# The recurrence over chunks of an RWKV-7 layer: products of one tile shape issued side by side, and longer pauses around them

## The chip, the core and the metric

One core of one Trainium2 chip runs the whole program. The metric is the device time of one execution in microseconds (us). Three executions of the kernel before are given: 1921.01, 1919.91 and 1916.69 us, median 1919.91 us.

A core has engines that run side by side, each of them in its own instruction order: TensorE (PE) multiplies matrices from SBUF into PSUM banks, VectorE (DVE) and ScalarE (ACT) work on SBUF and PSUM, GpSimd (POOL) does a few small things here, and SyncE (SP) starts the DMAs. They wait for each other by semaphores.

## The reference

Two layers follow each other, each as x + RMSNorm(mixer(RMSNorm(x))), with 256 tokens of 2048 features, all in float32. Layer 0 mixes by an RG-LRU and an mLSTM. Layer 1, where the change is, mixes by RWKV-7:

```python
u = h @ w_in                                  # 2048 -> 4 * 4096: r, k, v, z
...
def step(S, inp):                             # one token, per head of 64 x 64
    r_t, w_t, k_t, v_t, kk_t, a_t = inp
    sa = jnp.einsum('bhvk,bhk->bhv', S, -kk_t)
    S = (S * w_t[:, :, None, :] + sa[..., None] * (kk_t * a_t)[:, :, None, :]
         + v_t[..., None] * k_t[:, :, None, :])
    return S, jnp.einsum('bhvk,bhk->bhv', S, r_t)
...
y = head_norm(y, H, RWKV_GN_EPS, gn_g, gn_b) + bonus
return (y * jax.nn.silu(z)) @ w_out           # 4096 -> 2048
```

There are 64 heads of 64 features. The kernel cuts the 256 tokens into 4 chunks of 64, so that each chunk is a set of small matrix products and only the state S passes from chunk to chunk.

## The kernel before, in words

**Two kinds of TensorE work.** The bulk is the four projections, w_in and w_out of both layers. Each float32 weight is split into a high part (`whi`, an ACT copy) and a rest (`wlo`, a DVE subtraction), and so is the activation (`hh`, `hl`). A piece of an input projection (`in_mms`, line 220) is 24 products of 128x128 by 128x256 into the `gb` banks: 16 with `whi`, 8 with `wlo`; eight pieces make one projection of 512 columns. I call these the stream. All that the mixers need besides, in the `mb` banks, is small.

**Layer 1 by groups.** The loop at line 1144 takes the 64 heads in 8 groups of 8 heads (index g). For each group it issues four projections in the order k, r, z, v. The mixer's steps of the group run beside them, and reach over into the projections of the next group: the recurrence of group g runs during k and r of group g + 1.

**What sets the order.** TensorE runs in program order (`InOrder`, line 101; its instructions carry lines 116 and 119). The class `Weave` (line 57) writes that order: after every 4 stream products it adds 0.44 to a counter (`tick`), and emits from four lanes the steps whose time has come. A mixer is a Python generator; `yield w` says how much of the counter passes before its lane goes on. After a step that issued TensorE products the next step waits for 0.4 more, so that between two steps' products there are at least 4 stream products. A lane holds generators in a queue: lane 0 `blocks` and `inverse`, lane 1 `scores`, `values`, `recur`, `final`, lane 2 the first `norm`, lane 3 `decay` and `keys`. `drain` empties a lane's generator at a point where its result is needed, with few or no stream products between its steps. `Behind` (line 122) holds ACT's and DVE's instructions behind the weight splits that were emitted ahead of them, so ACT and DVE, too, work in the order in which the steps were emitted.

**The steps that matter here.**

- `shifted` and `keys` (line 836): after the k projection ACT and DVE make `kt`, ACT squares it into `sq` (four ACTIVATEs), and TensorE sums it per head (`mb<-cs,sq`, 8 products 128x2). DVE then makes `Gn` and `kP`, ACT and DVE make `BK` (8 times xx, zz, and a product of both).
- `blocks` (line 876): 32 products 64x64, `mb<-AR,BK`, which read all of `BK`; then `inverse` (line 935), a long substitution on DVE (`tf`, `Tb`), ending in 32x32 products (`ZT,Aab` and `TT,ZT`).
- `scores` (line 900): DVE makes the right half of `AR` from `rt`; TensorE makes, for f = 0 to 3, 8 products of 64x128 tiles (`mb<-AR,BK`) and 4 transposes (`mb<-cs,BK`); DVE evacuates them to `At`, ACT to `BKt`.
- `recur` (line 1028), for c = 0 to 3: `wb` = At (A part) times `UV`, ACT copies it to `Ws`; `ub` = inverse times `Ws` (`mb<-Ws,TT`, 64x64 tiles), DVE scales it into `UV`; `sb` = `BKt` times `UV` (`mb<-UV,BKt`, 128x64 tiles), DVE updates the state `Sn`, ACT copies it to the next chunk's slot of `UV`; then the outputs `Yb` = At (R part) times `UV` (`mb<-UV,At`, 128x64) plus, for c > 0, `Rc` times the old state (`mb<-Sn,Rc`, 64x64). `wb` and the first part of `Yb` read alike in the profile, `mb<-UV,At`. Each of these is a set of 8 products.
- `norm` (line 1112): ACT copies `Yb` to `Yn` and squares it, DVE and POOL make the rate, DVE multiplies. It runs for chunks 0 and 1 in lane 2 as soon as chunk 1's outputs are issued, and for chunks 2 and 3 at the end of `recur`, which then turns the result with 8 transposes (`mb<-cs,Yn`) into `yT` and adds the bonus on DVE. `final` (line 1132) multiplies it with the gate (`zt`, DVE).

The `mb` banks are four. A step that allocates one waits until the last reader of that bank is done.

Of the kernel before, what the change touches and what calls it, by code (L numbers as in the profile page):

```python
# [13 lines left out]
P = 128  # L14
# [12 lines left out]
# columns of the packed per-feature vectors: (name, tiles)  # L27
# [18 lines left out]
# columns of the constant array  # L46
# [10 lines left out]
class Weave:  # L57
    """Steps of the mixers, emitted between the products of the projections. A step yields the amount of
    products that come before its lane goes on."""
# [41 lines left out]
class InOrder:  # L101
    """The tensor engine, issuing in the order of the program."""
# [19 lines left out]
class Behind:  # L122
    """An engine whose instructions follow, in its own order, the splits of the weights emitted before them."""
# [20 lines left out]
def two_layers(ctx, tc, x, gpost, cst, selc, v0, v1, w_in0, w_out0, w_in1, w_out1, lruw, qkvw,  # L144
# [36 lines left out]
    def keep_warm(n, b):  # L181
        """Products that keep the clock of the tensor engine up while it waits; nothing reads them."""
        for _ in range(n):
            pe.matmul(b, lhsT=ones[:, 0:P], rhs=ones, start=True, stop=True)
# [15 lines left out]
    # ---------------------------------------------------------------- products  # L200
    def split_w(raw, w=512, into=None):
        """Weights to their high part and the rest."""
# [17 lines left out]
    def in_mms(banks, hi, lo, pc, h, nft, tick):  # L220
        """One piece (two k-tiles) of an input projection: first what needs the high parts of the weights alone."""
# [17 lines left out]
    def in_proj(wsrc, h):  # L239
        """512 columns of an input projection, features on partitions: two banks of two tiles."""  # L240
        banks = [gbank(), gbank()]
        for pc in range(8):
            in_mms(banks, *split_w(load_w(wsrc[pc])), pc, h, 4, 0.44)
        return banks
# [10 lines left out]
    def out_proj(wsrc, get_y, evac, tick, finish, after, room=None):  # L255
        """Output projection, tokens on partitions; get_y(g): the two parts of k-tiles 4g..4g+3. The last
        pieces of the last chunk go token tile by token tile, so that what follows the first is covered."""
# [49 lines left out]
    # ---------------------------------------------------------------- norms, tokens on partitions  # L307
    def rstd(ss):
        """ss [P, 4]: partial sums of squares of a token tile -> [P, 1]."""
# [10 lines left out]
    def scale(ss, pool_):  # L320
        """diag(rstd) of a token tile: transposes by products with it are scaled."""
# [4 lines left out]
    def to_features(xs, dg, g, warm):  # L326
        """Four tiles [P, 2, 512] of tokens, scaled by dg and g, to the two parts of h."""
        banks = {}
# [34 lines left out]
    def log1p_of(e, tmp):  # L363
        """log(1 + e), 0 <= e <= 1, as 2 atanh(e / (2 + e)); tmp: three tiles like e."""
# [12 lines left out]
    def silu2(banks, sz):  # L377
        """sz = 2 silu of two banks."""
# [6 lines left out]
    def residual(layer, tile_of):  # L385
        """The evacuation of out_proj: sums of squares, and the products with the post-norm's weights."""
# [17 lines left out]
    # ================================================================ layer 0  # L404
    with ExitStack() as l0:
# [35 lines left out]
        # small tables  # L441
# [37 lines left out]
        # ------------------------------------------------------------ mLSTM inputs  # L479
# [6 lines left out]
        def mlstm_in(c, xm):  # L486
# [43 lines left out]
            # both gates: two column tiles side by side, summed at the end  # L530
# [104 lines left out]
        # ------------------------------------------------------------ RG-LRU  # L635
# [70 lines left out]
        def room():  # L706
            """Parts of the weights in the place of what the heads have done with."""
# [18 lines left out]
    # ================================================================ layer 1  # L726
    with ExitStack() as l1:
# [19 lines left out]
        # derived per-feature vectors; the halves of the heads' partitions swap B and K  # L747
# [19 lines left out]
        def loras():  # L767
            """The first halves of the two loras: the token shift is taken after the product."""
# [35 lines left out]
        def decay(g, st):  # L804
            """What depends on the loras: the decay within chunks of 64 tokens, and the rate."""
# [481 lines left out]
```

## Time and profile before

| what | value |
|---|---|
| median of three executions | 1919.91 us (1916.69 to 1921.01) |
| span of the profiled execution, first to last instruction | 1912.7 us |
| PE busy | 1883.4 us, 98% of the span |
| PE weight loads busy | 1747.9 us, 91% |
| DVE busy | 1395.3 us, 73% |
| ACT busy | 1044.1 us, 55% |
| DMA, mean | 157 GB/s |
| mean granted TensorE clock | 0.997 |

The profile gives no time of its own for the profiled execution beside its span; the median of the runs lies 7.2 us above the span, the lowest run 4.0 us. One group of layer 1 takes about 131 us, which one reads from the same step of two neighbouring groups.

The rows of a timeline hold the start in us from the start of the span, the length in us, engine, line, operation, output<-inputs, TensorE's tile, the shape, how many instructions the row joins, and in brackets the idle time in front of it with what ended it. A float32 product shows as two records, so a set of 8 products is a row of x16. Lengths of neighbouring products overlap, so what a product costs is read from one start to the next.

### The profile page before, as it was taken

To read this page: it belongs to the slowest core of one execution; us is meant where nothing else is said; L and a number is where in the kernel's file an instruction comes from. 1 tells how busy PE (TensorE), PEld (TensorE's weight loads), DVE (VectorE), ACT (ScalarE), POOL (GpSimd) and SP (SyncE) were. 2 spreads that over 40 slices of the span, in tenths; PEclk is the share of its full clock that TensorE was granted. 3 is DMA by queue.
4 is the path that set the end of the run, shared out by engine and by line. 5 is a ranking of instruction groups with operands and counts; after the bars stand their busy time and mean duration, and the time that the engine had idled before them with its cause. 6 is when DMAs were issued, how large, how long until landed. Compare 5 with 4: busy or idle time off the path is not lost.

```text
span 1912.7 us, 39517 instructions
## 1 busy us (share of the span) xinstructions
PE 1883.4 (98%) x16498; PEld 1747.9 (91%) x16498; DVE 1395.3 (73%) x2302; ACT 1044.1 (55%) x1609; POOL 60.4 (3%) x84
## 2 busy tenths in 40 slices
PE   8999999999999999999999999999999999999998
PEld 7999999999888899989999999999999999997886
DVE  5667777757554569969689689597796896895544
ACT  5444666645444546555565555655655655555442
POOL 0000000000000100000000000000000000000000
PEclk9999999999999999999999999999999999999999
DMA  7433545455666444434444434344344443356664
GB/s 250 142 133 111 177 162 169 155 171 194 215 208 195 168 147 135 152 118 144 133 136 138 133 130 155 111 147 149 113 150 139 136 136 131 122 187 203 211 202 156
DMA packets 86947, 299.63 MB, mean 157 GB/s; under 512 B 9576, under 2 KB 12392, under 8 KB 86768
## 3 DMA queue, kind: packets, MB, share of 16 engines
q1 hardware_dynamic: 86768, 297.11, 47.2%
q8 instruction: 129, 2.11, 0.5%
q14 instruction: 50, 0.41, 0.1%
HBM read 289.20 MB, written 7.86 MB: 155 GB/s over the span
## 4 chain that ended last, share of the span: by engine, by line
PE 93%; DVE 4%; ACT 1%; issue 1%; DMA 0%; POOL 0%; SPq 0%; DVEq 0%; POOLq 0%; ACTq 0%
PE gb L116 75%; PE mb L116 17%; DVE wlo L132 2%; PE mb L119 1%; DVE wb L132 1%; ACT whi L132 1%; DMA xq<-in_x_dram 0%; DVE rt L132 0%; DVE Tb L132 0%; DVE tf L132 0%; DVE Ab L132 0%; DVE yT L132 0%; ACT ZT L132 0%; ACT vt L132 0%; DVE At L132 0%
## 5 line engine op out<-in xcount | busy, mean ns | idle before, releaser
L132 DVE TENSOR_TENSOR wlo<-raw,whi 128x1024 fp32r<-128x1024 f32 x509 | 619.9, 1219 | 338.0 <-ACT whi L132 304.5
L132 ACT CAST whi<-raw 128x1024 fp32r<-128x1024 f32 x509 | 532.6, 1048 | 557.3 <-PE gb L116 512.3
L116 PE MATMUL gb<-hh,whi 128*128 128x256 f32 x3120 | 790.5, 289 | 2.8 <-ACT whi L132 2.8
L116 PE MATMUL gb<-hl,whi 128*128 128x256 f32 x3120 | 770.6, 283 | 0.0
L116 PEld LDWEIGHTS gb<-hh,whi 128*128 128x128 f32 x3120 | 596.7, 191 | 13.6 <-ACT whi L132 3.7
L116 PEld LDWEIGHTS gb<-hl,whi 128*128 128x128 f32 x3120 | 597.5, 192 | 0.8
L116 PE MATMUL gb<-hh,wlo 128*128 128x256 f32 x3120 | 453.5, 286 | 0.0
L116 PEld LDWEIGHTS gb<-hh,wlo 128*128 128x128 f32 x3120 | 404.9, 191 | 4.2 <-issue 0.7
L116 PE MATMUL gb<-whi,yl 128*128 128x512 f32 x500 | 136.9, 392 | 0.5 <-DVE yl L132 0.5
L116 PE MATMUL gb<-whi,yh 128*128 128x512 f32 x500 | 136.5, 392 | 0.0
L116 PE MATMUL gb<-wlo,yh 128*128 128x512 f32 x500 | 135.7, 390 | 0.0
L116 PEld LDWEIGHTS gb<-whi,yl 128*128 128x128 f32 x500 | 93.2, 188 | 20.4 <-DVE yl L132 0.9
L116 PEld LDWEIGHTS gb<-wlo,yh 128*128 128x128 f32 x500 | 93.5, 188 | 19.8
L116 PEld LDWEIGHTS gb<-whi,yh 128*128 128x128 f32 x500 | 93.0, 188 | 19.3
L132 DVE TENSOR_TENSOR Tb<-Tb,tf 64x31 f32<-64x31 f32 (+15 forms) x248 | 82.6, 333 | 6.1
L132 DVE TENSOR_TENSOR tf<-Ab,Tb 64x31 f32<-64x31 f32 (+15 forms) x248 | 81.9, 330 | 4.5
L116 PE MATMUL mb<-AR,BK 64*128 64x128 f32 (+1 forms) x1024 | 58.0, 253 | 7.0 <-DVE AR L132 6.0
L116 PEld LDWEIGHTS mb<-AR,BK 64*128 64x128 f32 (+1 forms) x1024 | 50.2, 161 | 13.3 <-PE gb L116 7.1
L132 DVE TENSOR_TENSOR UV<-mb,Gn 64x256 f32<-64x256 f32 x64 | 26.9, 421 | 34.5 <-PE mb L116 33.4
L132 ACT ACTIVATE zz<-kP,dv 128x256 f32<-128x256 f32 x64 | 32.3, 505 | 22.9 <-DVE kP L132 12.4
L116 PEld LDWEIGHTS mb<-UV,At 128*64 128x64 f32 (+1 forms) x1024 | 35.0, 137 | 10.3 <-issue 2.5
L1125 POOL TENSOR_TENSOR vr<-vr,mhalf 128x8 f32<-128x8 f32 x16 | 28.3, 1771 | 499.4 <-DVE vr L132 499.4
(258 smaller groups left out, 1855.9 us busy)
## 6 DMA issues: line engine op xcount, KB each, us to landing
raw<-in_w_in_dram SPq DMA_DIRECT2D x384, 512.0 KB, 3.3
raw<-in_w_out_dram SPq DMA_DIRECT2D x128, 512.0 KB, 4.3
y1d<-zt SPq DMA_DIRECT2D x7, 512.0 KB, 3.9
yraw<-y1d SPq DMA_DIRECT2D x7, 512.0 KB, 4.3
l<-in_lora_dram SPq DMA_DIRECT2D x8, 384.0 KB, 4.6
xq<-in_x_dram SPq DMA_DIRECT2D x8, 256.0 KB, 5.2
lw<-in_lruw_dram SPq DMA_DIRECT2D x4, 512.0 KB, 4.6
xr<-in_x_dram SPq DMA_DIRECT2D x8, 256.0 KB, 6.0
```

What stands on the lines that cost most here:

```text
L116: return self._chain(self.eng.matmul(*a, **k))
L119: return self._chain(self.eng.transpose(**k))
L132: r = op(*a, **k)
L1125: pool.tensor_tensor(vr, vr, mhalf[:, 0:8], ALU.pow)
```

## The change

In `recur`, three things change. The product with `Rc` moves from behind the chunk's outputs to right behind `ub`, whose tile shape (64x64) it has, and now starts the sum in `Yb`; the two `Yb` banks are allocated there. The product of At's R part moves to right behind `sb`, whose tile shape (128x64) it has, and ends the sum. The pauses 2.4, 0.2 and 0.25 after the state update, the outputs and the `Rc` product become one of 3.8 after the state update (none after the last chunk). In `scores` the pause in front of the copy `Rc` and the score products grows from 2 to 3.4, and in `norm` the pause in front of the last multiplication from 1.74 to 2.6. The counter's pauses of one recurrence then sum to 24.2 instead of 21.55.

```diff
@@ -1044,18 +1044,27 @@
                 Ws = g1.tile([P, 4, 64], F32, name="Ws", tag="Ws", bufs=1)
                 act.copy(Ws, wb[:, 0:256].rearrange("p (f v) -> p f v", f=4))
                 yield 1.4
                 ub = mbank()
                 for f in range(4):
                     for hd in range(2):
                         hr = slice(64 * hd, 64 * hd + 64)
                         pe.matmul(ub[hr, f * 64:(f + 1) * 64], lhsT=TTv[hr, f, 0, c, :], rhs=Ws[hr, f, :],
                                   start=(f == 0), stop=True, skip_group_check=True)
+                if c % 2 == 0:
+                    Yb = [mbank(), mbank()]
+                cr = [slice(64 * ((c + hd) % 2), 64 * ((c + hd) % 2) + 64) for hd in range(2)]
+                if c:
+                    for f in range(4):
+                        for hd in range(2):
+                            hr = slice(64 * hd, 64 * hd + 64)
+                            pe.matmul(Yb[hd][cr[hd], f * 64:(f + 1) * 64], lhsT=Rc[hr, f, c, :],
+                                      rhs=St[hr, f, :], start=(f == 0), stop=False, skip_group_check=True)
                 for hd in range(2):
                     hr = slice(64 * hd, 64 * hd + 64)
                     dve.tensor_tensor(UV[hr, c, :, hd, :], ub[hr, 0:256].rearrange("p (f v) -> p f v", f=4),
                                       Gn[hr, :, c:c + 1].broadcast_to([64, 4, 64]), MUL)
                 yield 1.8
-                Sp = St
                 if c < 3:
                     sb = mbank()
                     for f in range(4):
@@ -1063,6 +1072,13 @@
                             hr = slice(64 * hd, 64 * hd + 64)
                             pe.matmul(sb[hr, f * 64:(f + 1) * 64], lhsT=BKt[:, f, c, hr], rhs=UV[:, c, f, hd, :],
                                       start=(f == 0), stop=True, skip_group_check=True)
+                for f in range(4):
+                    for hd in range(2):
+                        pe.matmul(Yb[hd][cr[hd], f * 64:(f + 1) * 64], lhsT=At[:, f, hd, c, 64:128],
+                                  rhs=UV[:, c, f, hd, :], start=(c == 0 and f == 0),
+                                  stop=True, skip_group_check=True)
+                if c < 3:
                     Sn = g1.tile([P, 4, 64], F32, name="Sn", tag="Sn", bufs=2)
                     sv = sb[:, 0:256].rearrange("p (f v) -> p f v", f=4)
                     pcb = PC[:, :, c:c + 1].broadcast_to([P, 4, 64])
@@ -1075,30 +1091,13 @@
                         hr = slice(64 * hd, 64 * hd + 64)
                         act.copy(UV[hr, c + 1, :, hd, :], Sn[hr])
                     St = Sn
-                    yield 2.4
-                if c % 2 == 0:
-                    Yb = [mbank(), mbank()]
-                cr = [slice(64 * ((c + hd) % 2), 64 * ((c + hd) % 2) + 64) for hd in range(2)]
-                for f in range(4):
-                    for hd in range(2):
-                        pe.matmul(Yb[hd][cr[hd], f * 64:(f + 1) * 64], lhsT=At[:, f, hd, c, 64:128],
-                                  rhs=UV[:, c, f, hd, :], start=(f == 0),
-                                  stop=(c == 0), skip_group_check=True)
-                yield 0.2
-                if c:
-                    for f in range(4):
-                        for hd in range(2):
-                            hr = slice(64 * hd, 64 * hd + 64)
-                            pe.matmul(Yb[hd][cr[hd], f * 64:(f + 1) * 64], lhsT=Rc[hr, f, c, :],
-                                      rhs=Sp[hr, f, :], start=False, stop=True, skip_group_check=True)
-                    yield 0.25
+                    yield 3.8
                 if c == 1:
                     nm = wv_.add(norm(0, Yb, Yn, Yn[:, 1]), 2)
...
             for f in range(4):
                 dve.tensor_tensor(AR[:, f, :, 64:128], c4(rt[:, f, :]), Pe[:, 4 * f:4 * f + 4, 1:65], MUL)
                 yield 0.5
-            yield 2
+            yield 3.4
             Rc = gt("Rc", "Rc", (4, 4, 64))
             act.copy(Rc, AR[:, :, :, 64:128])
...
             dve.tensor_scalar(vr, vr, 1.0 / 64.0, GN1_EPS, MUL, ADD)
             pool.tensor_tensor(vr, vr, mhalf[:, 0:8], ALU.pow)
-            yield 1.74
+            yield 2.6
             dve.tensor_tensor(yo, yo, vr.unsqueeze(2).broadcast_to([P, 8, 64]), MUL)
             yield 0.68
```

The rest of the diff removes comments, and lines shift by one.

The planner's order moves with it. First TensorE, where the recurrence of group 4 meets the k projection's end and the r projection of group 5: `mb<-UV,At` is `wb` or an output set, `mb<-cs,sq` the sums of the keys, `gb` the stream. Before, from chunk 1's outputs on:

```order
L116 MATMUL mb<-UV,At 64x64 x8
L116 MATMUL gb<-hh,whi 128x256
L116 MATMUL gb<-hl,whi 128x256
...
L116 MATMUL mb<-Sn,Rc 64x64 x8
...
L116 MATMUL mb<-UV,At 64x64 x8
L116 MATMUL gb<-hh,wlo 128x256 x8
L116 MATMUL mb<-cs,sq 128x2 x8
...
L116 MATMUL mb<-Ws,TT 64x64 x8
```

After, from chunk 1's state update on, which stands in the middle of the last `wlo` products of k:

```order
L116 MATMUL gb<-hh,wlo 128x256 x4
L116 MATMUL mb<-UV,BKt 64x64 x8
L116 MATMUL mb<-UV,At 64x64 x8
L116 MATMUL gb<-hh,wlo 128x256 x4
...
L116 MATMUL gb<-hh,wlo 128x256 x8
L116 MATMUL mb<-cs,sq 128x2 x8
...
L116 MATMUL mb<-UV,At 64x64 x8
...
L116 MATMUL mb<-Ws,TT 64x64 x8
L116 MATMUL mb<-Sn,Rc 64x64 x8
```

State update and outputs, and `ub` and the `Rc` set, now stand without stream products between them. From the end of k to `cs,sq` there were 24 stream products and three small sets (At, Rc and chunk 2's `wb`); now there are the same 24 stream products and no small set.

Second ACT, at the same place, where `sq` is made and the copies of the first `norm` (`Yn`) meet it. Before:

```order
L132 COPY UV<-Sn 64x4x64 x2
L132 ACTIVATE kt<-gb,dv_6640 128x256 x3
L132 ACTIVATE sq<-kt,vec_81 128x256
L132 ACTIVATE kt<-gb,dv_6640 128x256
L132 ACTIVATE sq<-kt,vec_81 128x256
L132 CAST whi<-raw 128x1024
L132 ACTIVATE sq<-kt,vec_81 128x256 x2
L132 COPY Ws<-mb 128x256
L132 COPY Yn<-mb 128x4x64
L132 COPY Yn<-mb 64x4x64 x2
L132 ACTIVATE Yn<-Yn 128x512
```

After, behind the first `kt`:

```order
L132 COPY Yn<-mb 128x4x64
L132 COPY Yn<-mb 64x4x64
L132 ACTIVATE kt<-gb,dv_6640 128x256
L132 COPY UV<-Sn 64x4x64 x2
L132 ACTIVATE kt<-gb,dv_6640 128x256
L132 ACTIVATE sq<-kt,vec_81 128x256
...
L132 CAST whi<-raw 128x1024
L132 ACTIVATE kt<-gb,dv_6640 128x256
L132 ACTIVATE sq<-kt,vec_81 128x256 x2
L132 ACTIVATE Yn<-Yn 128x512
L132 ACTIVATE sq<-kt,vec_81 128x256
```

The three copies and the square of `Yn` stood behind the fourth `sq`; now all four stand ahead of it (one copy is in the row left out).

Third DVE, behind the r projection of group 5, where `AR` is made for the scores. Before, with the inverse's steps (`tf`, `Tb`) between:

```order
L132 SCALAR_TENSOR_TENSOR rt<-gb,vec_81,rt 128x255
L132 TENSOR_TENSOR tf<-Ab,Tb 64x112
L132 SCALAR_TENSOR_TENSOR rt<-gb,vec_81,rt 128x255
L132 TENSOR_TENSOR Tb<-Tb,tf 64x28x4
L132 TENSOR_TENSOR AR<-rt,Pe 128x4x64
L132 TENSOR_TENSOR wlo<-raw,whi 128x1024
```

After:

```order
L132 TENSOR_TENSOR wlo<-raw,whi 128x1024
L132 TENSOR_TENSOR yT<-yT,vt 128x512 x2
L132 SCALAR_TENSOR_TENSOR rt<-gb,vec_81,rt 128x255 x2
L132 TENSOR_TENSOR wlo<-raw,whi 128x1024
L132 SCALAR_TENSOR_TENSOR rt<-gb,vec_81,rt 128x255 x2
L132 SCALAR_TENSOR_TENSOR zt<-yT,zt 128x4x128
L132 TENSOR_TENSOR wlo<-raw,whi 128x1024
L132 SCALAR_TENSOR_TENSOR zt<-yT,zt 128x4x128
L132 TENSOR_TENSOR AR<-rt,Pe 128x4x64 x4
```

The previous group's bonus and gate (`yT`, `zt`) were done ahead of the first `rt`; now the two `yT` stand right ahead of it and both `zt` between `rt` and the first `AR`. On TensorE the first score set stood 40 stream products behind the end of r; now it stands 72 behind it.

## The prediction, as put on record

> **What bounds the kernel now.** I read the page's busy shares and the chain of waits first:
>
> ```profile
> span 1912.7 us, 39517 instructions
> PE 1883.4 (98%) x16498; PEld 1747.9 (91%) x16498; DVE 1395.3 (73%) x2302; ACT 1044.1 (55%) x1609; POOL 60.4 (3%) x84
> PE gb L116 75%; PE mb L116 17%; DVE wlo L132 2%; PE mb L119 1%; DVE wb L132 1%; ACT whi L132 1%; DMA xq<-in_x_dram 0%; DVE rt L132 0%; DVE Tb L132 0%; DVE tf L132 0%; DVE Ab L132 0%; DVE yT L132 0%; ACT ZT L132 0%; ACT vt L132 0%; DVE At L132 0%
> ```
>
> TensorE sets the end: it is busy for 98% of the span, and the small sets of the mixers (`mb`) are 17% of the chain. A change helps by what it takes off TensorE and hurts by every us for which TensorE stands still. The table of TensorE's waits shows how little that is now:
>
> ```profile
> PE mb L116 <- DVE AR L132: 6.0, 6, 1.0
> PE mb L116 <- ACT ZT L132: 1.6, 5, 0.3
> PE mb L116 <- ACT sq L132: 1.0, 2, 0.8
> PE mb L116 <- DVE BK L132: 0.8, 1, 0.8
> ```
>
> So in layer 1 TensorE stands about 9 us in all. But the low figures don't mean slack. TensorE's timeline where the recurrence of group 4 meets the k projection's end:
>
> ```profile
> 1350.25 1.11 PE L116 MATMUL gb<-hh,wlo 128*128 128x256 f32 x8
> 1351.20 0.28 PE L116 MATMUL gb<-hh,whi 128*128 128x256 f32 x1
> ...
> 1352.05 0.28 PE L116 MATMUL gb<-hl,whi 128*128 128x256 f32 x1
> 1352.25 0.69 PE L116 MATMUL mb<-UV,At 128*64 128x64 f32 x16
> 1352.87 0.39 PE L116 MATMUL gb<-hh,whi 128*128 128x256 f32 x1
> 1353.09 0.28 PE L116 MATMUL gb<-hl,whi 128*128 128x256 f32 x1
> ...
> 1353.54 0.68 PE L116 MATMUL mb<-Sn,Rc 64*64 64x64 f32 x16
> ...
> 1356.49 1.84 PE L116 MATMUL mb<-cs,sq 128*128 128x2 f32 x16
> ```
>
> ACT in the same stretch:
>
> ```profile
> 1351.45 0.83 ACT L132 COPY UV<-Sn 64x256 f32<-64x256 f32 x2
> 1352.30 0.84 ACT L132 ACTIVATE kt<-gb,dv 128x256 f32<-128x256 f32 x2
> ...
> 1354.45 0.50 ACT L132 ACTIVATE sq<-kt,vec 128x256 f32<-128x256 f32 x1
> 1354.92 1.05 ACT L132 CAST whi<-raw 128x1024 fp32r<-128x1024 f32 x1
> 1355.88 0.91 ACT L132 ACTIVATE sq<-kt,vec 128x256 f32<-128x256 f32 x2
> 1356.69 0.35 ACT L132 COPY Ws<-mb 128x256 f32<-128x256 f32 x1
> 1356.94 1.14 ACT L132 COPY Yn<-mb 128x256 f32<-128x256 f32 x3
> 1358.11 0.63 ACT L132 ACTIVATE Yn<-Yn 128x512 f32<-128x512 f32 x1
> ```
>
> The last `sq` ends at 1356.79, 0.3 us into the set that reads it: just in time, with nothing to spare.
>
> **What the merging takes off TensorE.** The stream goes at 0.12 us per product (1351.20 to 1352.05, seven of them). From the start of the product at 1352.05 to that at 1353.09 are 1.04 us with two stream products (0.24), so a lone set of 8 inserts 0.80. How much of it is the products themselves? A set four times as long, elsewhere, and the one that is next behind it:
>
> ```profile
> 845.29 2.08 PE L116 MATMUL mb<-AR,BK 64*64 64x64 f32 x64
> 847.30 0.74 PE L116 MATMUL gb<-hh,wlo 128*128 128x256 f32 x4
> ```
>
> From start to next start, 64 records take 2.01 us and 16 take 0.62 (1352.25 to 1352.87), so 48 more cost 1.39, 0.029 each, and 16 cost 0.46. The other 0.34 is paid once per set, for leaving the stream's tile shape and coming back. Per group of heads three At sets go behind `sb` and three Rc sets behind `ub`; the fourth At set keeps its place as a set of its own. That is 6 x 8 = 48 times 0.34, **-16.4 us**, on the engine that bounds. [...]
>
> One wait goes as well: chunk 2's `sb` takes 1.05 against the At set's 0.69, because its `UV` comes late.
>
> ```profile
> 1361.09 1.05 PE L116 MATMUL mb<-UV,BKt 128*64 128x64 f32 x16
> ```
>
> Six groups by 0.36: **-2.2** (0 if the wait only moves to the merged pair).
>
> **cs,sq.** From the end of k to this set TensorE had 24 stream products and three small sets, 5.29 us (1351.20 to 1356.49). Now it has the 24 alone, 2.9 us. ACT's work in that stretch grows instead: by the order of its rows, from the first `kt` to the last `sq` stand four `kt` (0.42), two copies `UV<-Sn` (0.83 both), four `sq` (0.46), one `whi` (1.05) and, new, three `Yn` copies (1.14) and the `Yn` square (0.63): 1.68 + 0.83 + 1.84 + 1.05 + 1.14 + 0.63 = 7.2 us. The set needs the first `sq` at its start and the others 0.46 apart (1.84 for four), so its last quarter may start at 2.9 + 1.4 = 4.3 and gets its `sq` at 7.2: it stands 2.9 us. At the least 1.7: the first `kt`'s bank is done 4 products, 0.5 us, before the end of k, and the lengths of neighbouring rows overlap by up to 0.1 (1354.92 and 1355.88), 0.7 over twelve. I take 2.3 for groups 2 to 7: **+14** (10 to 17). Group 1's set stands 1.0 already, which stays.
>
> **AR.** The rows of DVE and TensorE behind the end of r (1388.47, where the stream's next piece starts):
>
> ```profile
> 1387.51 1.12 PE L116 MATMUL gb<-hh,wlo 128*128 128x256 f32 x8
> 1388.47 0.28 PE L116 MATMUL gb<-hh,whi 128*128 128x256 f32 x1
> ...
> 1394.43 1.16 PE L116 MATMUL mb<-AR,BK 64*128 64x128 f32 x16 [1.00 <-DVE AR L132]
> ```
>
> ```profile
> 1386.97 0.69 DVE L132 TENSOR_TENSOR yT<-yT,vt 128x512 f32<-128x512 f32 x1
> 1387.70 0.69 DVE L132 SCALAR_TENSOR_TENSOR zt<-yT,zt 128x512 f32<-128x512 f32 x1
> 1388.68 1.21 DVE L132 TENSOR_TENSOR wlo<-raw,whi 128x1024 fp32r<-128x1024 f32 x1
> 1392.71 0.48 DVE L132 SCALAR_TENSOR_TENSOR rt<-gb,vec,rt 128x255 f32<-128x255 f32 x1
> 1393.87 0.41 DVE L132 TENSOR_TENSOR AR<-rt,Pe 128x256 f32<-128x256 f32 x1
> 1395.34 0.86 DVE L132 SCALAR_TENSOR_TENSOR rt<-gb,vec,rt 128x255 f32<-128x255 f32 x2
> ```
>
> DVE is behind here: it reaches the first `rt` 4.24 us after r's end and has the first `AR` 1.57 later, 5.81, while TensorE, 40 products on, is there at 4.8: the 1.0 us of the bracket. The longer pause and the later queue of lane 1 put TensorE's set 72 products behind r, 8.64 us. But from the first `rt` to the first `AR` DVE now has four `rt` (1.7), two `wlo` (2.4), two `zt` (1.4) and `AR` (0.4), 5.9 us, and two `yT` (1.4) ahead of them. If it is at the first `rt` after 4.24 us as now, `AR` is ready at 10.1, 1.5 late; if it is at `yT` then, at 11.5, 2.9 late. The middle, 2.2, is 1.2 more than now, six times: **+7.2** (-6.0 if DVE keeps up, to +11).
>
> **The first drain of scores.** In front of v of group 1 the order now leaves two score sets with four stream products between them and the set before, and none between each other; before, those sets were out by then. A set takes three of the four banks, so the next one stands until two `At` on DVE (each as long as `yT`, 0.69) and the `wlo` (1.2) between them are done, 2.6 us, of which TensorE covers 0.5 to 1 with what is left of its own: about 2 us for each of two sets, **+4** (0 to 5.2). It happens once.
>
> **BK and ZT.** Blocks stands on the last `BK` already:
>
> ```profile
> 1374.74 2.30 PE L116 MATMUL mb<-AR,BK 64*64 64x64 f32 x64
> ...
> 1375.88 0.42 DVE L132 TENSOR_TENSOR BK<-xx,zz 128x256 f32<-128x256 f32 x1 [1.90 <-ACT zz L132]
> ```
>
> 2.30 against 2.08 above. Between `cs,sq` and blocks three of the merges come to lie (3 x 0.34) and the 0.36 of `sb` goes: TensorE gets there up to 1.4 us sooner, `BK`'s chain on ACT and DVE doesn't. What `cs,sq` stood before counts against it. I take 0.8 by six, **+4.8** (0 to 8.4). The wait for `ZT` (0.3, five times) is of the same kind: DVE and ACT lead, and the scores' DVE work is bunched nearer to it. I take 0.5 more each, **+2.5** (0 to 5). Single waits for `Ws` and for the first `yl` of the output projection: +0.6 (0 to 3). DMA, SP and POOL are untouched: the weight loads keep their order, and the store of `zt` moves by a few loads in SP's.
>
> **Sum.** -16.4 - 2.2 + 14 + 7.2 + 4 + 4.8 + 2.5 + 0.6 = **+14.5 us**. On the profiled span of 1912.7 that is 1927.2; the median of the runs, 1919.9, lies 7.2 above that span, and with it the forecast is **1934.4 us**.
>
> **The rivals.** *The pauses do it* (faster). If ACT gets the copies of `Yn` and the `sq` done while TensorE still streams, and DVE is not behind at `AR`, then `cs,sq`, `BK` and `ZT` cost nothing new and the AR wait goes: -16.4 - 2.2 - 6.0 + 4 = -20.6, 1899.3. It decides at one point: whether the last `sq` is done within 4.3 us after k's end. For it: ACT is 55% busy and may run ahead. Against: the row at 1355.88 says that it was just in time with 2.4 us more and four instructions fewer. A middle case, where half of the `cs,sq` term, the drain and 2 us of the rest come and AR stays as it is, gives -16.4 - 2.2 + 7 + 4 + 2 = -5.6, 1914.3. I give the full case 0.10 and the middle one 0.09.
>
> *No change.* The merges are paid back by `cs,sq` and the drain alone: -16.4 - 2.2 + 14 + 4 = -0.6, 1919.3. I give it 0.11.
>
> *The clock.* In layer 1 the granted clock falls once, behind a stretch of 32x32 products with a wait:
>
> ```profile
> 1585.00:1588.00 3.00, 2.69 (x69) 2.45 (x68) 2.94 (x7) 2.95 (x5) 0.00 (x0) 1.00 0.75 253
> 1588.00:1591.40 3.40, 3.40 (x18) 3.40 (x18) 0.78 (x1) 1.64 (x3) 0.00 (x0) 0.51 0.53 174
> ```
>
> 3.4 us at half speed cost 1.7. If each new stand of 2 us and more set it off (six at `cs,sq`, six at AR), 12 x 1.7 = 20 more: 1955. [...] That it fell in one of five such groups speaks against a dozen. I give it 0.06.
>
> *It isn't the tile shape.* If the 0.34 belonged to every set and its banks rather than to the change of shape, the merges would bring nothing and the sum be +31: 1951. Against it: the 64 records of blocks write two banks in one shape and pay it once. I give it 0.02.
>
> **The numbers.** The forecast has 0.62, the clock 0.06, not the shape 0.02: slower 0.70. No change has 0.11; 0.2%, 3.8 us, is about what a measurement of this kernel can tell. Faster has 0.10 + 0.09 = 0.19. The forecast's own bounds are `cs,sq` 10 to 17, AR -6 to 11, `sb` -2.2 to 0, the drain, `BK`, `ZT` and the rest together 0 to 21.6; they don't all fall to one side, and its likely part is 1922 to 1948. The range goes down from there through the cases of no change and of the middle, to 1906, and leaves out the full gain, the clock and not the shape, 0.18: 1906 to 1948.
>
> **What would show it.** In the profile after: sets x32 of one shape where `ub` and Rc, `sb` and At stand, 48 of them; the wait for `sq` in the table of TensorE's waits at 10 us or more in place of 1.0; for `AR` near 13 in place of 6.0; TensorE's busy time and its stands together 15 us longer, of which the stands are up by some 30. I am wrong if `sq` stays under 3, or if the x32 sets insert twice 0.8.

## The result and the profile after

The changed kernel takes 1949.39 us (median of 4 executions, 1948.55 to 1951.21) against 1918.54 us for the kernel before, measured beside it: a ratio of 1.0163, 95% interval 1.0151 to 1.0175. It is slower by 31 us. The profiled span grew from 1912.7 to 1949.4 us, by 36.7, and the mean granted clock fell from 0.997 to 0.978. The spans differ by more than the medians because the profiled execution of the kernel before had a high clock for that kernel: of 66 executions of it that were measured beside the runs below, the four at a clock of 0.997 took 1914.8 us on average, the 27 at 0.994 took 1919.8 and the two at 0.992 took 1922.2.

The page and the chain after:

```profile
span 1949.4 us, 39523 instructions
PE 1893.9 (97%) x16497; PEld 1766.7 (91%) x16498; DVE 1396.1 (72%) x2302; ACT 1043.0 (54%) x1609; POOL 65.1 (3%) x84
PE 91%; DVE 4%; ACT 3%; issue 1%; DMA 0%; POOL 0%; SPq 0%; DVEq 0%; POOLq 0%; ACTq 0%
```

TensorE does fewer changes of shape and yet is busy for 10.5 us longer; ACT's share of the chain went from 1% to 3%. The table of TensorE's waits after:

```profile
PE mb L116 <- DVE AR L132: 18.6, 6, 3.1
PE mb L116 <- ACT sq L132: 11.0, 14, 1.3
PE mb L116 <- DVE At L132: 2.8, 3, 2.2
PE mb L116 <- ACT ZT L132: 1.6, 5, 0.3
PE mb L116 <- DVE BK L132: 0.8, 1, 0.8
```

AR went from 6.0 to 18.6 and sq from 1.0 to 11.0; ZT and BK didn't move. TensorE at the place that the prediction showed, the end of k in group 5 (stream rows left out):

```profile
1374.57 0.69 PE L116 MATMUL mb<-UV,BKt 128*64 128x64 f32 x16
1375.08 0.64 PE L116 MATMUL mb<-UV,At 128*64 128x64 f32 x16
1375.65 0.74 PE L116 MATMUL gb<-hh,wlo 128*128 128x256 f32 x4
...
1378.15 1.12 PE L116 MATMUL gb<-hh,wlo 128*128 128x256 f32 x8
1379.11 0.51 PE L116 MATMUL mb<-cs,sq 128*128 128x2 f32 x4
1380.91 1.05 PE L116 MATMUL mb<-cs,sq 128*128 128x2 f32 x8 [1.30 <-ACT sq L132]
1382.34 0.61 PE L116 MATMUL mb<-cs,sq 128*128 128x2 f32 x4 [0.37 <-ACT sq L132]
...
1385.57 0.41 PE L116 MATMUL gb<-hh,whi 128*128 128x256 f32 x1
1386.00 0.41 PE L116 MATMUL gb<-hh,whi 128*128 128x256 f32 x1
```

The merged pair is there, and the merge pays: from 1374.57 to the stream's next start at 1375.65 both sets take 1.08 us, where two lone ones took 1.24 (0.62 each) and went over to their shape and back twice. With the way there the pair inserts 1.27 us into the stream, two lone sets 1.62. The set for the keys stands twice, 1.67 us together. And three us later the stream runs at 0.43 for two products instead of 0.24. ACT in that stretch:

```profile
1375.19 0.47 ACT L132 ACTIVATE kt<-gb,dv 128x256 f32<-128x256 f32 x1
1375.76 0.77 ACT L132 COPY Yn<-mb 128x256 f32<-128x256 f32 x2
1376.55 0.48 ACT L132 ACTIVATE kt<-gb,dv 128x256 f32<-128x256 f32 x1
1376.92 0.81 ACT L132 COPY UV<-Sn 64x256 f32<-64x256 f32 x2
...
1378.66 0.36 ACT L132 COPY Yn<-mb 64x256 f32<-64x256 f32 x1
1379.05 1.05 ACT L132 CAST whi<-raw 128x1024 fp32r<-128x1024 f32 x1
...
1381.16 0.62 ACT L132 ACTIVATE Yn<-Yn 128x512 f32<-128x512 f32 x1
1381.78 0.51 ACT L132 ACTIVATE sq<-kt,vec 128x256 f32<-128x256 f32 x1
```

ACT has no pause in it; the norm's copies and its square stand between the keys' steps. At AR, DVE and the set that waits for it:

```profile
1418.84 1.28 DVE L132 TENSOR_TENSOR yT<-yT,vt 128x512 f32<-128x512 f32 x2
1420.15 0.87 DVE L132 SCALAR_TENSOR_TENSOR rt<-gb,vec,rt 128x255 f32<-128x255 f32 x2
...
1424.59 0.68 DVE L132 SCALAR_TENSOR_TENSOR zt<-yT,zt 128x512 f32<-128x512 f32 x1
1425.19 1.42 DVE L132 TENSOR_TENSOR AR<-rt,Pe 128x256 f32<-128x256 f32 x4
```

```profile
1425.75 2.08 PE L116 MATMUL mb<-AR,BK 64*128 64x128 f32 x16 [3.09 <-DVE AR L132]
1427.76 1.11 PE L119 MATMUL mb<-cs,BK 128*128 128x128 f32 x4
```

The stand is 3.09 us where it was 1.00, and behind it the same 16 records take 2.08 instead of 1.16 and the transposes 1.11 instead of 0.66. The windows around both places, with the granted clock in the third column from the right:

```profile
1380.57:1383.98 3.41, 2.69 (x22) 2.48 (x22) 3.18 (x9) 1.72 (x4) 0.00 (x0) 1.00 0.44 154
1383.98:1387.39 3.41, 3.41 (x28) 3.29 (x28) 1.65 (x4) 1.57 (x4) 1.64 (x1) 0.50 0.02 7
1387.39:1390.81 3.42, 3.42 (x51) 3.13 (x50) 2.86 (x7) 2.65 (x5) 0.00 (x0) 1.00 0.00 0
```

```profile
1421.53:1424.94 3.41, 1.13 (x10) 0.92 (x8) 3.41 (x6) 1.88 (x3) 0.00 (x0) 1.00 0.43 155
1424.94:1428.35 3.41, 2.60 (x19) 2.40 (x20) 3.41 (x8) 1.04 (x1) 0.13 (x1) 0.50 0.77 217
1428.35:1431.76 3.41, 3.41 (x18) 3.41 (x17) 2.96 (x8) 0.59 (x1) 0.00 (x0) 0.50 0.65 244
1431.76:1435.17 3.41, 3.41 (x36) 3.15 (x36) 1.89 (x3) 1.43 (x2) 0.00 (x0) 1.00 0.02 5
```

Behind the first of these two stands TensorE ran at half its clock for 3.41 us (0.50 in the second window), at the other one for twice that. In the groups of layer 1 the trace after has 20 such intervals in 14 places; the trace before had one. In groups 2 to 7 there are twelve of these stands, six of 1.67 us at `cs,sq` and six of 3.1 us at `AR`; half clock follows eleven of them. Behind the twelfth, 3.11 us in front of the score set at 1017.09, the clock stays full.

Where the 36.7 us come from, by what each kind of set inserts into the stream (from the start of the stream product ahead of it to that of the second stream product behind it, less what these two take by themselves: 0.12 each, or 0.227 beside the 512 columns of the output projection; summed over the timeline):

| | before | after | difference |
|---|---|---|---|
| sets of the recurrence | 119.2 | 105.2 | -14.0 |
| `cs,sq` | 15.6 | 28.4 | +12.8 |
| score sets | 62.6 | 85.8 | +23.2 |
| blocks, `ZT,Aab`, `TT,ZT` | 59.9 | 59.1 | -0.8 |
| the remainder: the stream itself and the rest of the program | | | +15.5 |

The remainder is the stream at half clock, for the most part. Of the score sets' 23.2 us, 12.6 are the longer wait for `AR` and 4.8 belong to two sets that are drained in group 1; the other 5.8 come from sets that run at half clock.

### The profile page after: what moved, and what is told of

It reads as the page before. It is cut to its first block, busy times and chain, and to the rows that moved or that the text cites. A ratio compares the mean times of both kernels' runs of the same rounds, so it can differ in the third digit from the quotient of the medians.

```text
span 1949.4 us, 39523 instructions
## 1 busy us (share of the span) xinstructions
PE 1893.9 (97%) x16497; PEld 1766.7 (91%) x16498; DVE 1396.1 (72%) x2302; ACT 1043.0 (54%) x1609; POOL 65.1 (3%) x84
## 4 chain that ended last, share of the span: by engine, by line
PE 91%; DVE 4%; ACT 3%; issue 1%; DMA 0%; POOL 0%; SPq 0%; DVEq 0%; POOLq 0%; ACTq 0%
PE gb L116 74%; PE mb L116 16%; PE mb L119 2%; DVE wlo L132 1%; ACT whi L132 1%; ACT sq L132 1%; ACT Yn L132 0%; DVE At L132 0%; DVE Ab L132 0%; DVE zt L132 0%; DVE Tb L132 0%; ACT UV L132 0%; ACT kt L132 0%; DVE tf L132 0%; DMA xq<-in_x_dram 0%
## 5 line engine op out<-in xcount | busy, mean ns | idle before, releaser
L116 PE MATMUL gb<-hh,whi 128*128 128x256 f32 x3120 | 803.1, 293 | 2.8 <-ACT whi L132 2.8
L116 PE MATMUL gb<-hl,whi 128*128 128x256 f32 x3120 | 782.6, 286 | 0.0
L116 PEld LDWEIGHTS gb<-hh,whi 128*128 128x128 f32 x3120 | 608.2, 195 | 12.2 <-ACT whi L132 3.6
L116 PEld LDWEIGHTS gb<-hl,whi 128*128 128x128 f32 x3120 | 608.8, 195 | 0.8
L116 PE MATMUL mb<-AR,BK 64*128 64x128 f32 (+1 forms) x1024 | 61.7, 265 | 22.3 <-DVE AR L132 18.6
L1124 POOL TENSOR_TENSOR vr<-vr,mhalf 128x8 f32<-128x8 f32 x16 | 32.5, 2033 | 484.9 <-DVE vr L132 484.9
L132 ACT COPY BKt<-mb 128x512 f32<-128x512 f32 x32 | 18.8, 588 | 53.6 <-PE mb L119 53.6
L116 PE MATMUL mb<-UV,At 128*64 128x64 f32 (+1 forms) x1024 | 46.0, 235 | 0.1
```

Of the source, the lines that this page charges most:

```text
L116: return self._chain(self.eng.matmul(*a, **k))
L132: r = op(*a, **k)
L1124: pool.tensor_tensor(vr, vr, mhalf[:, 0:8], ALU.pow)
```

## The experiments

Two things were to be told apart: is it the order that the pauses make (theory A: TensorE stands at `AR` and `cs,sq`, and the clock falls behind long stands, while the merges by themselves save 16 us), or the merges themselves (rival M)? And does the clock's share come from the stands, or from elsewhere (rival C)? Each ratio is against the kernel before on the same chip. That kernel's median was 1917.5 to 1919.8 us there, so 1 or 2 us between two experiments say little.

### Both merges, the old pauses

```diff
-                    yield 3.8
+                    yield 2.85
...
-            yield 3.4
+            yield 2
             Rc = gt("Rc", "Rc", (4, 4, 64))
...
-            yield 2.6
+            yield 1.74
```

> The changed kernel with the merges kept and the old pauses put back (2.85 in one piece after the state update, 2 before the scores, 1.74 in the norm). Theory A (the order that the longer pauses make lets TensorE stand at AR and at cs,sq, and each long stand is followed by stretches at half clock; the merges by themselves save 16 us): the AR wait falls from 18.6 us to about the 6 of before, the sq wait stays near 11 to 15 because the sets that lay in front of it are still gone, dips of the clock fall from 14 in layer 1 to about 6, all at cs,sq: 1922 to 1935 us. Rival M (the merges themselves cost the time, by banks held longer or by the sets standing side by side): it stays at 1940 to 1950 us.

Measured 1924.92 us, ratio 1.0034 (1.0023 to 1.0045). The waits:

```profile
PE mb L116 <- ACT sq L132: 11.2, 14, 1.2
PE mb L116 <- DVE AR L132: 6.1, 6, 1.0
```

AR is back at the 6 of before, sq stays, as theory A has it. 24 of the 31 us are the pauses' doing. But the merges with the old pauses still lose 7 us: what they save is more than eaten by `cs,sq`, which lost the sets in front of it, and by the clock behind it (14 intervals at half clock in eight places of layer 1, seven of them behind `cs,sq`).

### The longer pauses alone

```diff
-                    yield 2.4
+                    yield 3.35
                 # outputs of this chunk
...
-            yield 2
+            yield 3.4
             Rc = gt("Rc", "Rc", (4, 4, 64))
...
-            yield 1.74
+            yield 2.6
```

> The kernel before with the longer pauses alone (the sum after the state update 3.8, the scores 3.4, the norm 2.6) and no merge. Theory A: the long stand at AR comes back with its dips of the clock, nothing is saved: slower than the changed kernel by about the 16 us of the merges, 1955 to 1975 us. Rival M: close to the kernel before, under 1928 us.

Measured 1960.76 us, ratio 1.0223 (1.0197 to 1.0248): within theory A, and 11 us above the changed kernel. The pauses do harm without any merge, and on top of them the merges help. The waits:

```profile
PE mb L116 <- DVE AR L132: 16.0, 6, 2.7
PE mb L116 <- ACT sq L132: 9.7, 8, 1.5
```

So the longer pauses alone bring the stand at `cs,sq`, too, with all the small sets unmerged. The merges with the old pauses bring it as well (11.2); in the changed kernel it is 11.0, not the sum, so neither edit can be called its only cause.

### Each pause by itself, on both merges

Each of three kernels keeps one of the longer pauses and has the other two as before: 3.8 behind the state update, 3.4 ahead of the scores, 2.6 in the norm.

> Merges kept, the pause after the state update longer (3.8), the scores and norm pauses as before. Theory A says that this pause is what makes the recurrence end later, so that the scores, which share its lane, and the previous group's last DVE steps (yT, zt) meet behind the end of r: the AR wait is back at 15 us or more with dips of the clock behind it, 1940 to 1955 us, at least two thirds of the 24 us between the old pauses (1925) and the changed kernel (1949). Rival S (the pause in front of the scores does it, since it moves them most directly): within 6 us of the 1925.

> Merges kept, the pause in front of the scores longer (3.4), the other two as before. Theory A: a small part, AR wait up by no more than 6 us, 1925 to 1937 us; the longer pause gives DVE time ahead of the first set and takes it away between the sets. Rival S: most of the 24 us, over 1941 us.

> Merges kept, the pause in the norm longer (2.6), the other two as before. Theory A: almost nothing, since this step's engines are not waited for nearby, 1923 to 1930 us. Rival N (the norm's later end moves yT and zt behind r): AR wait over 12 us, over 1936 us.

Measured 1944.24 us (ratio 1.0128, 1.0113 to 1.0144), 1931.48 us (1.0069, 1.0054 to 1.0084) and 1926.02 us (1.0039, 1.0025 to 1.0053). Over the 1924.92 of the old pauses these are 19, 7 and 1 us, together 27, against 24.5 for all three at once; the last 1 us is no more than chips differ by. The times lie in theory A's ranges in all three, and in its rivals' in none. The state update's pause is the one that matters, and its AR wait shows why, though it is short of the 15 us that theory A had:

```profile
PE mb L116 <- DVE AR L132: 13.6, 6, 2.3
```

The recurrence ends later, and `scores`, queued in its lane, is emitted behind it and behind `final`, whose `zt` then stand ahead of `AR` on DVE. With the scores' pause alone the wait for `AR` is not in the table of waits at all; the pause does what its place suggests there, and time is lost later: the second to fourth score sets of a group insert 2.2 to 2.3 us each, where with the old pauses they insert 1.7 to 1.8. Over the timeline the score sets cost 4.4 of the 6.6 us. That they follow each other faster than DVE empties their banks is the likely reason; the table of waits shows only 1.7 us of it.

### Filling the stands of the changed kernel

```diff
+                for _ in range((10, 0, 3, 0)[f] if g > 1 else 0):
+                    pe.matmul(b[:, 256:512], lhsT=ones[:, 0:P], rhs=ones[:, 0:256], start=False, stop=True, skip_group_check=True)
...
+                if f == 0 and g > 1:
+                    keep_warm(11, ab[0])
```

> The changed kernel with products that nothing reads put where TensorE stands in groups 2 to 7: ten of 128x256 and three more inside cs,sq, eleven of 128x512 in front of the first score set. They fill 1.1, 0.3 and 2.4 us of stands of 1.3, 0.4 and 3.1 us. Theory A, its part on the clock (a stand is what the half clock follows): the dips in groups 2 to 7 go, the mean granted clock rises from 0.978 to 0.99 or more, and the time falls by 15 to 25 us, to 1924 to 1935 us, with the same waits. Rival C (the clock falls for another reason, such as the mixture of small products, or at random): clock 0.975 to 0.982, the time 1947 to 1955 us.

Measured 1942.56 us, ratio 1.0127 (1.0107 to 1.0147), clock 0.994. The clock came back as theory A said: six intervals at half clock in five places, not 20 in 14. The time did not: 6.8 us less, and neither range holds it. Its waits say where the rest went:

```profile
PE mb L116 <- DVE At L132: 6.2, 14, 2.3
PE mb L116 <- DVE BK L132: 4.6, 7, 0.8
PE mb L116 <- DVE AR L132: 3.8, 6, 0.6
```

At full speed TensorE comes sooner to the next things that DVE and ACT owe it: BK rose from 0.8 to 4.6 and At from 2.8 to 6.2, together 7.2 us. So a part of the slow clock had only stood where TensorE would have waited; the 14 intervals were 24 us of lost clock, and these two waits do not account for all that did not come back. The last two groups of this run have no half clock at all and take 134.7 us from one blocks set to the next, where the kernel before takes 131.2 and the changed one 135.3 to 138.1 in groups 2 to 7. Most of what a group lost is there at full clock, too: it is the stands, filled or not.

### Filling the stand of the merges with the old pauses

The same with ten products in front of `cs,sq` and four behind its first products, on the kernel with the old pauses.

> Merges with the old pauses, and in groups 2 to 7 ten products of 128x256 that nothing reads in front of cs,sq and four more inside it, where TensorE stands 1.2 and 0.5 us. Theory A: the dips of the clock at cs,sq (five of 3.4 us of lost clock, one of 1.7) go, the wait for sq all but goes, and as no other long wait stands close behind, most of the lost time comes back: 1908 to 1918 us. Rival C (the lost clock lies where TensorE would wait for ACT and DVE anyway): 1921 to 1927 us.

Measured 1921.72 us, ratio 1.0015 (1.0005 to 1.0024). This is rival C's range: no dip of the clock is left at `cs,sq` of groups 2 to 7, but 3 us come back. In the place of the wait for sq stands one for `Ws` that was not there:

```profile
PE mb L116 <- ACT Ws L132: 5.3, 6, 0.9
```

and the clock now falls behind `TT,ZT`, in five groups.

### One merge at a time

On the kernel before, with its pauses. First the At output set alone, moved behind the state update's set for chunks 0 to 2:

```diff
+                    for f in range(4):
+                        for hd in range(2):
+                            pe.matmul(Yb[hd][cr[hd], f * 64:(f + 1) * 64], lhsT=At[:, f, hd, c, 64:128],
+                                      rhs=UV[:, c, f, hd, :], start=(f == 0),
+                                      stop=(c == 0), skip_group_check=True)
```

> The kernel before with one of the two merges: the At output set behind the state update's set for chunks 0 to 2; Rc sets and pauses as before. Theory A: three changes of tile shape per group go (24 x 0.35 = -8 us); as the Rc set still stands between the end of k and cs,sq, TensorE comes there about 0.8 us sooner than ACT now, so a small sq wait of 0 to 0.6 us per group, no dips of the clock in most groups: 1909 to 1918 us, that is 1 to 9 us under the kernel before. Rival M (merged sets hold the banks or starve the stream): no gain or slower, 1919 to 1930 us.

Then the Rc set alone, moved behind the inverse's set for chunks 1 to 3:

```diff
+                if c:
+                    for f in range(4):
+                        for hd in range(2):
+                            hr = slice(64 * hd, 64 * hd + 64)
+                            pe.matmul(Yb[hd][cr[hd], f * 64:(f + 1) * 64], lhsT=Rc[hr, f, c, :],
+                                      rhs=St[hr, f, :], start=(f == 0), stop=False, skip_group_check=True)
```

> The kernel before with the other merge: the Rc set behind the inverse's set for chunks 1 to 3; At sets and pauses as before. Theory A: as above, 24 x 0.35 to 0.5 = -8 to -12 us, less a wait for sq of up to 0.6 us per group: 1909 to 1919 us. Together with the run above: two single merges gain, both together (1925 us with the old pauses) lose, because only both together take all small sets out of the stretch that ACT needs in front of cs,sq. Rival M: the loss of 7 us of both merges divides among them, 1919 to 1926 us each.

At alone: 1919.52 us, ratio 1.0009 (0.9997 to 1.0020), a miss for theory A by 1.5 us and inside rival M's range. Rc alone: 1912.26 us, ratio 0.9955 (0.9937 to 0.9972), faster than the kernel before. The waits for sq are 2.1 and 2.4 us here against 11.2 with both: one small set left in front of `cs,sq` is all but enough for ACT. ACT's order is part of it: with one merge the square of `Yn` and its last copy run behind the last `sq` again, and the experiments don't separate this from the set that is left. Why the gains are smaller than the sums of the merges shows in Rc's trace, by the blocks sets of five groups:

```profile
982.22 2.41 PE L116 MATMUL mb<-AR,BK 64*64 64x64 f32 x64
1114.98 2.41 PE L116 MATMUL mb<-AR,BK 64*64 64x64 f32 x64
1247.73 2.41 PE L116 MATMUL mb<-AR,BK 64*64 64x64 f32 x64
1377.40 2.41 PE L116 MATMUL mb<-AR,BK 64*64 64x64 f32 x64
1507.10 2.41 PE L116 MATMUL mb<-AR,BK 64*64 64x64 f32 x64
```

Two groups take 132.8 us and two 129.7. The first two have two intervals of half clock each, the others none; outside these intervals their sets insert the same. A group without them is 1.5 us under the 131.2 of the kernel before, one with them 1.6 above. In At's trace it is the same, 132.8 and 130.2, so half clock accounts for At's miss, and rival M isn't needed for it: At's groups without half clock are faster than before. How many groups have it changes from execution to execution: the seven of Rc alone took 1903.82 us at a clock of 0.998 to 1913.45 at 0.993.

### A few products more, on the faster kernel

```diff
+                for _ in range(3 if f == 0 else 0):
+                    pe.matmul(b[:, 256:512], lhsT=ones[:, 0:P], rhs=ones[:, 0:256], start=False, stop=True, skip_group_check=True)
...
             tb = [mbank(), mbank()]
+            for _ in range(4):
+                pe.matmul(tb[0][:, 0:256], lhsT=ones[:, 0:P], rhs=ones[:, 0:256], start=True, stop=True, skip_group_check=True)
```

> The kernel with the Rc merge alone, and per group three products of 128x256 that nothing reads behind the first of the cs,sq products and four in front of the TT,ZT set, where TensorE stands 0.24 and 0.3 us; they take about 0.11 us each, 0.2 us per group more than the stands. In the run without them, groups with a dip of the clock took 132.8 us and groups without one 129.7. [...]

> The same with six and six products, about 0.75 us per group more than the stands cover. Theory A: no dip in groups 2 to 7, but the products cost up to 6 us themselves: 1905 to 1912 us, the clock at 0.995 or more. Rival C: 1915 to 1921 us with dips as before.

> A control: the kernel before, unmerged, with the same three and four products per group that nothing reads. Theory A: it had one dip of the clock in layer 1, so there is at most 1.7 us to gain and about 2 us of added products: 1916 to 1922 us, and the gain of the Rc merge with these products is the merge's. If instead the added products help by themselves (by changing what is waited for), it is under 1913 us.

Rc with three and four products: 1905.58 us, ratio 0.9931 (0.9917 to 0.9944); with six and six: 1909.09 us, 0.9949 (0.9937 to 0.9962); the kernel before with three and four: 1916.89 us, 0.9986 (0.9977 to 0.9995). In both Rc kernels the clock is 0.997 and no interval at half clock is left in groups 2 to 7. The larger number of products took 3.5 us more. The control is faster by 0.14%, 2.9 us, within the expected range though clear of the noise. Its groups take 131.4 us, no less than the 131.2 of the profiled kernel before; what it gains is the clock of the other executions, a median of 0.997 where the kernel before has 0.994 beside it. The expected 1.7 us at most took the one profiled execution for all of them. The Rc merge's own part is what lies between, 1905.6 against 1916.9, 11 us (129.8 against 131.4 per group), near the upper end of the 8 to 12 that the changes of shape gave for it. What the added products do on top is to make the half clock rare: the five executions with three and four have a mean clock of 0.996 to 0.998, where Rc alone has 0.992 to 0.998. Without them one execution of Rc alone was as fast, at 1903.82. The first of these is the fastest version found by its median, 0.7% under the kernel before and 2.2% under the changed one.

## Why the prediction was wrong, point by point

The side was right and the size was not: 1934.4 us forecast, range 1906 to 1948, 1949.4 measured. The prediction's own sign says where to look. It had TensorE's stands up by some 30 us and stands and busy time together up by 15, so that the busy time would fall by about 15. The stands rose by 26.2 (29.3 to 55.5), near enough; the busy time rose by 10.5. TensorE did the same work more slowly, and the forecast had nothing for that. The sizes by term, of the profiled spans:

- *The merges, -16.4, and the wait at chunk 2's `sb`, -2.2.* Right: the recurrence's sets insert 14.0 us less, and 17.5 less (119.2 to 101.7) in the run with the stands filled, where few of them run at half clock. `UV` is not in the table of waits beyond 0.3.
- *`cs,sq`, +14.* Right: +12.8, of which the wait is 10.0. The 1.67 us in group 5 lie at the lower bound, 1.7, where ACT starts early, as it did (its first `kt` at 1375.19, before k's last product).
- *AR, +7.2.* Too small, the second step that failed. The wait rose by 12.6. In group 5 the first score set was due 3.09 before 1425.75, less the change of shape, and with 72 products (8.64 us) in front of it r ended near 1413.9. DVE reached `yT` at 1418.84, 4.9 us later: `yT`, not the first `rt`, came at the old lag of 4.24 and a little over. That was the upper of the two cases, a stand of 2.9, and 3.09 came; the middle was taken.
- *The first drain, +4.* About right: its two sets inserted 8.8 against 4.0 before, +4.8, a part of it at half clock.
- *BK +4.8 and ZT +2.5.* Neither came: 0.8 and 1.6 as before. The stand at `cs,sq` and the slow clock kept TensorE from getting there sooner. The BK term was not invented, though: with the stands filled BK stands at 4.6.
- *The clock, nothing in the sum.* This is the step that failed most. "That it fell in one of five such groups speaks against a dozen" gave 0.06 to the rival that came about, and nothing to the forecast itself. Measured are +15.5 in the stream, 5.8 in the score sets and 3.5 in the recurrence's (14.0 against 17.5). The one in five was read from a single execution, and one with a high clock for its kernel; 62 of the 66 other executions have 0.992 to 0.996. Nor did a stand of 0.3 us say what a longer one does: half clock followed one of five stands of 0.3 us behind thin products, none of the kernel before's six stands of 1.0 us at `AR`, and eleven of the twelve new ones of 1.67 and 3.1. The rival's place was right but for one stand and its 1955 us close. Its price of 12 x 1.7 = 20 us came near by luck: there were 20 intervals, 34 us of lost clock, and a part of them ran while TensorE stood or would have stood.

What the forecast took to be additive is not: as the filled stands show, taking away 14 of the 20 slow intervals brought 6.8 us, in part because DVE and ACT used the slow time to catch up (the waits for `BK` and `At` rose by 7.2 us). How much the clock takes by itself therefore has no single number here: with the stands left as they are it is about 25 of the 36.7 by which the spans differ, with the stands filled 6.8. That the pauses and the merges cause the stands, and that the slow intervals go when the stands are filled, was shown; why they follow one stand or set of thin products and not another was not.

## What to carry to other kernels

When TensorE is the bound and its order is planned by hand, each small set in front of a consumer is also the time that another engine needs for its input: before sets are merged or moved, look for the place where that engine was just in time, and leave one set in front of it (here the waits for `sq` were 2.1 and 2.4 us with one set left and 11.2 with none). Merge one kind at a time and read the other engines' order again after each; pauses tuned for one order are not right for the next. And price a stand of TensorE in a dense kernel with what its clock does afterwards, not by its length alone: here half clock of 3.41 or 6.83 us followed eleven of the twelve stands of 1.67 and 3.1 us. Read that clock from several executions: the one that was profiled may be among the best, as here, with 0.997 where 62 of 66 others had 0.992 to 0.996.

## What the runs showed of the hardware

In four traces, between the end of layer 0 and the program's last microseconds, the half clock came in stretches of 3.41 us or twice that. The 32 starts of these stretches are, in each trace, whole multiples of 3.4133 us apart, within 0.02 us: in the kernel before both lie at 0.90 us past a multiple (652.85 and 1588.10), in the changed one all 15 at 1.58, in Rc alone all seven at 3.13, in At alone all eight at 1.50. Two windows of the Rc run, laid on these multiples, show that the page's busy share doesn't tell which one half clock follows. Both have a `cs,sq` set and its stand of 0.24 us in them; one is followed by half clock and the other isn't:

```profile
1228.52:1231.93 3.41, 3.17 (x36) 2.95 (x36) 2.96 (x9) 3.03 (x7) 0.00 (x0) 1.00 0.15 32
1231.93:1235.34 3.41, 3.41 (x38) 3.29 (x33) 3.14 (x6) 1.00 (x2) 0.00 (x0) 0.50 0.33 127
...
1358.24:1361.65 3.41, 3.17 (x35) 3.01 (x29) 3.12 (x7) 3.41 (x8) 0.00 (x0) 1.00 0.40 147
1361.65:1365.06 3.41, 3.41 (x52) 3.20 (x52) 2.93 (x9) 1.88 (x5) 0.00 (x0) 1.00 0.51 159
```

Both are busy for 3.17 us. But in the first the set lies whole (1228.80 to 1230.9) with only 0.28 us of stream ahead of it, in the second 1.7 us of stream come first and the set begins at 1359.96. In the kernel before, half clock followed a window that was busy for 3.10 us, with 32x32 tiles in it (1584.69 to 1588.10). And a longer stand was not always followed by it. The changed kernel's stand of 3.11 us at 1017.09 lies across two such windows, busy for 2.05 and 1.66 us, and no half clock follows either:

```profile
1011.92:1015.33 3.41, 2.05 (x18) 1.85 (x16) 3.41 (x7) 2.74 (x4) 0.00 (x0) 1.00 0.49 179
1015.33:1018.74 3.41, 1.66 (x21) 1.56 (x22) 3.41 (x7) 0.70 (x1) 0.13 (x1) 1.00 0.73 197
1018.74:1022.16 3.42, 3.42 (x33) 3.29 (x34) 3.32 (x9) 1.88 (x3) 0.00 (x0) 1.00 0.89 337
```

Pairs of sets with 64x64 tiles inserted the least. Of the changed kernel's 24 pairs of `ub` and Rc nine insert 1.10 to 1.12 us and six 1.21 or 1.22, with their records interleaved in the trace, and the other nine 1.27 or more; of its 24 pairs of `sb` and At the least is 1.27, where two lone sets insert 1.62.
